# Moving the row split of the last output stores from tiles 58 and 59 to tile 48, in a one-core matmul with bias and residual

## The chip, the cores and the metric

The kernel runs on one core of one Trainium2 chip. The metric is the device time of one execution in microseconds (us). The kernel before was at 210.7 us (median of 3 runs, 210.52 to 210.83) when the prediction was made.

## The reference

```python
# x: (16, 512, 1024), weight: (1024, 768), bias: (768,), residual: (16, 512, 768), all float32
def reference(x, weight, bias, residual):
    return (np.matmul(x, weight) + bias + residual).astype(np.float32)
```

The 8,192 rows of the result are worked on as 64 tiles of 128 rows. The output is 25.17 MB, the inputs 61.88 MB.

## The kernel before

TensorE transposes and multiplies tile after tile, VectorE adds, and SyncE issues all DMA transfers from one list, in order. Each entry waits until what it needs is done. A transfer is shared out over DMA engines; the moment at which the trace records that one engine's share is done is called a landing (16 of them for each plain store of 128 rows). "Engine" with a number below is a DMA engine. The cuts of the code are marked with dots.

```python
# ORDER: kind, group S of 16 tiles, first tile, end tile[, row to cut at]
# x: load of x, r: load of residual, s: store of finished tiles, c: half of the last tile
ORDER = [ ...
 ('r', 2, 6, 16), ('s', 1, 0, 16), ('x', 3, 0, 6), ('r', 3, 0, 7), ('x', 3, 6, 16),
 ('r', 3, 7, 16), ('s', 2, 0, 16), ('s', 3, 0, 10), ('s', 3, 10, 12, 108), ('s', 3, 12, 14),
 ('s', 3, 14, 15), ('c', 3, 15, 0), ('c', 3, 15, 1)]
...
            else:                                    # a store
                n0, nl = (0, N) if kind == "s" else LAST[j1]
                j1 = j1 if kind == "s" else j0 + 1
                edges = [0, *cut, P]                 # P = 128
                for p0, p1 in zip(edges, edges[1:]):
                    K_(nc.sync.dma_start(
                        out=out_d[S, p0:p1, j0:j1, n0:n0 + nl],
                        in_=R[p0:p1, (J * S + j0) % RR:(J * S + j0) % RR + j1 - j0, n0:n0 + nl],
                    ))
```

A store of several tiles has one packet per row of SBUF, of 3,072 bytes times the number of tiles: the three stores of 16 tiles are 384 packets of 49,152 bytes in the trace, the ten-tile store 128 of 30,720. Shared equally, a plain store of 128 rows gives 8 packets to each of the 16 DMA engines, as the packet chains of the prediction have it. The entry `('s', 3, 10, 12, 108)` cuts tiles 58 and 59 into 108 rows and 20 rows, so that the engines carry different amounts: in the trace the 108-row store has 12 landings and the 20-row store 10. Eight of those 10 come 0.44 to 0.48 us, about two 6 KB packets, after one of the 12.

No trace gives an engine's number. The numbers used here are names: 0 to 9 are the ten engines of the 20-row store, 10 and 11 the other two of the 108-row store, 12 to 15 the rest. That rows are shared equally, and that a part with fewer landings always uses the lower names, are assumptions.

So engines 0 to 9 carry 9 + 2 = 11 rows of tiles 58 and 59, engines 10 and 11 carry 9, and engines 12 to 15 none.

Of the kernel before, what the change touches and what calls it, by code (L numbers as in the profile page):

```python
# [32 lines left out]
 ('r', 0, 6, 16), ('x', 0, 14, 16), ('x', 1, 0, 6), ('r', 1, 0, 6), ('x', 1, 6, 16),  # L33
 ('r', 1, 6, 16), ('s', 0, 0, 16), ('x', 2, 0, 6), ('r', 2, 0, 6), ('x', 2, 6, 16),
 ('r', 2, 6, 16), ('s', 1, 0, 16), ('x', 3, 0, 6), ('r', 3, 0, 7), ('x', 3, 6, 16),
 ('r', 3, 7, 16), ('s', 2, 0, 16), ('s', 3, 0, 10), ('s', 3, 10, 12, 108), ('s', 3, 12, 14),
 ('s', 3, 14, 15), ('c', 3, 15, 0), ('c', 3, 15, 1)]
LAST = [(0, 512), (512, 256)]


# [256 lines left out]
```

## Time and profile before

| | before |
|---|---|
| median of the timed runs | 210.7 us |
| the profiled execution | 211.16 us, span 209.4 us |
| last VectorE add ends | 204.48 us |
| last store (128 KB) issued, landed | 204.51, 208.30 us |

The page of the kernel before, some lines of its parts 1, 3 and 4:

```profile
span 209.4 us, 3113 instructions
...
PE 202.3 (97%) x1298; PEld 130.3 (62%) x1298; DVE 104.7 (50%) x140; ACT 66.1 (32%) x69; POOL 115.9 (55%) x72
...
q1 hardware_dynamic: 4766, 87.05, 97.6%
q8 instruction: 10, 0.16, 0.3%
q14 instruction: 4, 0.03, 0.0%
...
PE 92%; DMA 4%; ACT 1%; DVE 1%; SPq 0%; issue 0%
```

TensorE is busy for 97% of the span and the DMA engines for 97.6%. The packets of the two queues that the page calls "instruction" are called fetches here. Those of q8 are ten packets of 16,384 bytes, 17 to 20 us apart. They share engines with the data (all ten begin 3 to 4 ns before the end of a data packet): in the packet records a data packet ends at 196.02 us just where the fetch of 196.01 us begins, and the next data packet follows the fetch at 197.06.

What SyncE waited for from 195 us on (us in total, times, longest):

```profile
SPq L130 <- DVE ro L199: 6.1, 2, 4.4
SPq L292 <- DMA out_dram<-ro: 3.5, 1, 3.5
```

The second line is the end of the kernel: 3.5 us in which nothing is left but stores. The timeline near the end (start, us, engine and line):

```profile
200.44 4.40 SPq L130 DMA_DIRECT2D out_dram<-ro  x4
...
203.25 1.23 DVE L262 TENSOR_TENSOR ro<-psum_o,ro 128x512 f32<-128x512 f32 x2 [0.77 <-PE psum_o L258]
```

The last four transfers are issued from 200.44 us on, each as soon as its tile is added. The same stretch by 2 us windows:

```profile
core 0: us, PE busy (x) PEld busy (x) DVE busy (x) ACT busy (x) POOL busy (x), PEclk, DMA share, GB/s
200.00:202.00 2.00, 2.00 (x14) 1.13 (x12) 0.89 (x2) 0.00 (x0) 0.00 (x0) 1.00 0.73 270
202.00:204.00 2.00, 2.00 (x14) 1.08 (x12) 1.18 (x2) 0.00 (x0) 0.00 (x0) 1.00 1.01 416
204.00:206.00 2.00, 0.02 (x1) 0.00 (x0) 0.42 (x1) 0.00 (x0) 0.00 (x0) 1.00 0.92 365
206.00:208.00 2.00, 0.00 (x0) 0.00 (x0) 0.00 (x0) 0.00 (x0) 0.00 (x0) 1.00 0.25 92
```

The DMA share is 0.73 at 200 to 202 us, when some engines have run dry, and 0.25 after 206 us, when only the late ones still work.

### The profile page before, as it was taken

How to read it: one execution, taken by the hardware profiler on the slowest of the kernel's cores; microseconds unless marked ns; L12 is line 12 of the kernel's file. 1: busy time of each engine (PE TensorE's matmuls, PEld its weight loads, DVE VectorE, ACT ScalarE, POOL GpSimd, SP SyncE). 2: the span in 40 equal slices, each digit the busy share in tenths (PEclk: the TensorE clock that was granted, in tenths of full speed). 3: DMA queues.
4: the chain of work that ended last, by engine and by line, in shares of the span. 5: the costliest groups of instructions: out<-in, count | busy, mean ns of one | idle time of the engine just before them, and what ended most of it. 6: DMA issues, size and time to landing. Idle time of an engine off the chain costs nothing.

```text
span 209.4 us, 3113 instructions
## 1 busy us (share of the span) xinstructions
PE 202.3 (97%) x1298; PEld 130.3 (62%) x1298; DVE 104.7 (50%) x140; ACT 66.1 (32%) x69; POOL 115.9 (55%) x72
## 2 busy tenths in 40 slices
PE   7999999999999999999999999999999999999990
PEld 2455666666666666666666666666666666666650
DVE  0448555445544554554455454645544554554460
ACT  2444513312730371310460083320180065330000
POOL 2100039769999806997049603999009940799200
PEclk9999999999999999999999999999999999999998
DMA  6999999999989899899999999999999999998984
GB/s 232 426 425 429 428 433 457 393 464 410 472 378 495 383 494 415 385 415 444 408 435 479 408 417 474 441 412 390 424 476 399 459 407 449 451 441 384 415 354 166
DMA packets 4780, 87.24 MB, mean 417 GB/s; under 512 B 538, under 2 KB 666, under 8 KB 1694
## 3 DMA queue, kind: packets, MB, share of 16 engines
q1 hardware_dynamic: 4766, 87.05, 97.6%
q8 instruction: 10, 0.16, 0.3%
q14 instruction: 4, 0.03, 0.0%
HBM read 61.88 MB, written 25.17 MB: 416 GB/s over the span
## 4 chain that ended last, share of the span: by engine, by line
PE 92%; DMA 4%; ACT 1%; DVE 1%; SPq 0%; issue 0%
PE psum_o L164 78%; PE pt L157 13%; DMA x_tile<-in_x_dram 4%; PE psum_o L258 1%; ACT xb L146 1%; DVE xt L158 0%; DVE ro L262 0%; SPq L119 0%; SPq L122 0%
## 5 line engine op out<-in xcount | busy, mean ns | idle before, releaser
L164 PE MATMUL psum_o<-w_sb,xt 128*128 128x512 bf16 x1008 | 174.0, 326 | 0.3 <-DVE xt L158 0.3
L164 PEld LDWEIGHTS <-xt 128*128 128x128 bf16 x1008 | 98.5, 98 | 59.0 <-DVE xt L158 0.7
L189 POOL TENSOR_TENSOR ro<-ro,bias_sb 128x768 f32<-128x768 f32 x50 | 88.9, 1822 | 48.0 <-DMA ro<-in_residual_dram 37.4
L149 ACT CAST xb<-x_tile 128x1024 bf16<-128x1024 f32 x60 | 59.7, 1043 | 113.8 <-DMA x_tile<-in_x_dram 62.7
L158 DVE COPY xt<-pt 128x1024 bf16<-128x1024 bf16 x64 | 44.0, 691 | 84.9 <-PE pt L157 84.8
L199 DVE TENSOR_TENSOR ro<-psum_o,ro 128x768 f32<-128x768 f32 x49 | 46.5, 948 | 4.3 <-POOL ro L189 3.2
L185 POOL TENSOR_TENSOR ro<-ro 128x768 f32<-128x768 f32 x14 | 25.0, 1815 | 25.1 <-DMA ro<-in_residual_dram 25.0
L157 PE MATMUL pt<-ident,xb 128*128 128x128 f32 x256 | 38.5, 274 | 0.2 <-ACT xb L146 0.2
L157 PEld LDWEIGHTS pt<-ident,xb 128*128 128x128 f32 x256 | 29.9, 142 | 9.0 <-ACT xb L146 1.1
L195 DVE TENSOR_TENSOR ro<-psum_o,bias_sb 128x768 f32<-128x768 f32 x14 | 13.2, 948 | 0.0
L208 PE MATMUL psum_o<-warm 128*128 128x512 bf16 x12 | 5.3, 632 | 1.2 <-DVE warm_a L204 1.2
L229 ACT CAST w_sb<-ro 128x768 bf16<-128x768 f32 x4 | 3.3, 832 | 3.7 <-DMA ro<-in_weight_dram 3.7
L208 PEld LDWEIGHTS <-warm 128*128 128x128 bf16 x12 | 1.6, 144 | 3.9 <-issue 2.8
L229 POOL CAST w_sb<-ro 128x768 bf16<-128x768 f32 x1 | 0.8, 822 | 5.5 <-DMA ro<-in_weight_dram 5.5
L149 DVE CAST xb<-x_tile 128x1024 bf16<-128x1024 f32 x1 | 0.7, 693 | 4.4 <-DMA x_tile<-in_x_dram 4.4
L146 ACT CAST xb<-x_tile 128x512 bf16<-128x512 f32 x3 | 1.8, 616 | 3.4 <-PE psum_o L164 1.7
L258 PE MATMUL psum_o<-w_sb,xt 128*128 128x512 bf16 (+1 forms) x16 | 2.8, 326 | 0.0
L229 DVE CAST w_sb<-ro 128x768 bf16<-128x768 f32 x3 | 1.7, 558 | 2.0 <-DMA ro<-in_weight_dram 2.0
L147 DVE CAST xb<-x_tile 128x512 bf16<-128x512 f32 x3 | 1.2, 424 | 2.4 <-DMA x_tile<-in_x_dram 2.4
L258 PEld LDWEIGHTS <-xt 128*128 128x128 bf16 x16 | 1.6, 98 | 1.1
L223 PE MATMUL psum_o<-warm 128*128 128x512 bf16 x6 | 1.6, 379 | 0.0
L262 DVE TENSOR_TENSOR ro<-psum_o,ro 128x512 f32<-128x512 f32 (+1 forms) x2 | 1.1, 558 | 0.9 <-PE psum_o L258 0.8
(14 smaller groups left out, 5.1 us busy)
## 6 DMA issues: line engine op xcount, KB each, us to landing
out_dram<-ro SPq DMA_DIRECT2D x3, 6144.0 KB, 34.1
x_tile<-in_x_dram SPq DMA_DIRECT2D x3, 5120.0 KB, 24.1
ro<-in_residual_dram SPq DMA_DIRECT2D x3, 3840.0 KB, 25.2
x_tile<-in_x_dram SPq DMA_DIRECT2D x3, 3072.0 KB, 40.2
ro<-in_residual_dram SPq DMA_DIRECT2D x3, 2304.0 KB, 17.5
x_tile<-in_x_dram SPq DMA_DIRECT2D x4, 1024.0 KB, 8.2
x_tile<-in_x_dram SPq DMA_DIRECT2D x2, 2048.0 KB, 21.0
out_dram<-ro SPq DMA_DIRECT2D x1, 3840.0 KB
```

The lines of the kernel that those rows point to most:

```text
L146: K_(nc.scalar.copy(out=dst[:, 0:K // 2], in_=src[:, 0:K // 2]))
L149: K_((nc.scalar.copy if how == "s" else nc.vector.tensor_copy)(out=dst, in_=src))
L157: K_(nc.tensor.transpose(out=pt[:, q, :], in_=words[:, ts(q, P)], identity=ident))
L158: K_(nc.vector.tensor_copy(out=XT[t % XT_N].rearrange("p q m e -> p (q m e)"), in_=pt.rearrange("p q m -> p (q m)").bitcast(BF16),))
L164: K_(nc.tensor.matmul(PO[t % HEAD][:, n0:n0 + nl], lhsT=XT[t % XT_N][:, q, :, e], rhs=w_sb[:, q, e, n0:n0 + nl], start=(q == 0 and e == 0) ...
L185: K_(nc.gpsimd.tensor_add(out=r, in0=r, in1=tmp(t)))
L189: K_(nc.gpsimd.tensor_add(out=r, in0=r, in1=bias_sb))
L195: K_(nc.vector.tensor_add(out=tmp(t), in0=p, in1=bias_sb))
L199: K_(nc.vector.tensor_add(out=row(t), in0=p, in1=row(t)))
L208: K_(nc.tensor.matmul(PO[0][:, 0:512], lhsT=warm[:, 0:P], rhs=warm, start=True, stop=True))
L229: K_(copy(out=w_sb[:, q, e, :], in_=w_st[:, 2 * q + e, :]))
L258: K_(nc.tensor.matmul(p, lhsT=XT[t % XT_N][:, q, :, e], rhs=w_sb[:, q, e, n0:n0 + nl], start=(q == 0 and e == 0), stop=(q == n_q - 1 and e ...
```

## The change

The intent is to balance the end differently. Tiles 58 and 59 go back to a plain store, so that no engine should run dry. The uneven cut moves to tile 48, which is ready long before its turn (its two parts are issued near 161 us): 100 rows on ten engines (10 each), 28 on fourteen (2 each), none on engines 14 and 15. The stores after it are grouped anew.

```diff
- ('r', 3, 7, 16), ('s', 2, 0, 16), ('s', 3, 0, 10), ('s', 3, 10, 12, 108), ('s', 3, 12, 14),
- ('s', 3, 14, 15), ('c', 3, 15, 0), ('c', 3, 15, 1)]
+ ('r', 3, 7, 16), ('s', 2, 0, 16), ('s', 3, 0, 1, 100), ('s', 3, 1, 9), ('s', 3, 9, 12),
+ ('s', 3, 12, 14), ('s', 3, 14, 15), ('c', 3, 15, 0), ('c', 3, 15, 1)]
```

## The prediction

> **What bounds the kernel.** The page gives TensorE 97% of the 209.4 us span, and the chain of waits is 92% TensorE. The change touches no compute, so the body (to 204 us) cannot move. Only the tail can: the timeline ends the last VectorE add at 204.48 us, and the last 128 KB store is issued at 204.51. The issue list puts its landing 3.8 us later, near 208.3; SyncE waits 3.5 us for it. So stores are still queued when compute ends.
>
> **Who is late.** I chained the DMA packet records (each packet starts where an earlier one ends), which gives 16 engines. All but four of them are busy without a gap from the large store of tiles 32-47 to the end. They differ: the ten-tile store (8 packets of 30,720 bytes, 1.138 us each) ends at 198.8-199.4 us on six engines, 200.2-200.7 on seven, 200.95 on one whose packets took 1.18 us (call it N), 201.97 and 202.10 on two that lost about 1.4 us to one 16 KB instruction fetch each (at 196.0 and 176.0 us; call the second P). [...]
>
> [...] the 108-row store has 12 landings, the 20-row one 10. P's landing is in the first (204.61 us) and not in the second (last 204.07), so P is engine 10 or 11. It got 9 rows of 6,144 bytes (0.2305 us each), and its last packet ends at 207.97, landing 208.30. N (one of 0-9, 11 rows) is next, ending at 207.43, then one at 207.02. Four engines (12-15) got none of tiles 58-59; three of them ran dry before the next store, issued at 200.44, reached them.
>
> **What the change does.** Bytes and issue of the last transfers stay; one transfer is added, issued near 161 us while SyncE idles. Estimated work of an engine between the store of tiles 32-47 and the end, from those packet times (3,072 bytes: 0.118 us):
> - before: engines 0-9 15.4 us, 10-11 14.9, 12-15 12.8 plus idling;
> - after: 0-9 15.2 us (12 rows of tile 48), 10-13 14.0 (2 rows), 14-15 13.8 (none).
>
> So P gains 0.9 us (to about 207.05), N 0.2 us (to about 207.25); the engine hit at 196 us, one of 12-15, ends at about 206.9 instead of 205.8. The latest is then N, 0.7 us earlier than P was. Everything of this lies on the critical path, but it is all there is[...].
>
> **Prediction.** 210.7 - 0.7 = 210.0 us, 209.5 to 210.6 at 8 in 10. Faster by over 2%: 0.01; within 2%: 0.98; slower: 0.01.
>
> **What would show it.** The last VectorE add still ends at 204.5 us; SyncE's last wait falls from 3.5 to about 2.8 us; last landing near 207.6; the landings of the last store span less than before (2.1 us); no engine is dry at 200-202 us, so the DMA share there, now 0.73, is near 0.95; P's last packet is 0.9 us earlier.
>
> **What would make it wrong.** The instruction fetches land on other engines or at other times, so that another engine (one of 0-9) is the late one and gains only 0.2 us; [...] (some 6 KB packets of the 108-row store took up to 0.9 us instead of 0.23); N slower than before; or unprofiled runs without these delays, where balance is different.

"Engine" numbers are the names given above, and how the rows divide over the engines was an assumption; the landing counts (12 and 10 before, 10 and 14 after) fit it.

## The result, and the profile after

The changed kernel took 210.73 us (median of 6 runs, 210.65 to 210.90), the kernel before 210.61 us beside it (6 runs, 210.50 to 210.83). The ratio is 1.0006, 95% interval 0.9993 to 1.0019: no difference. The predicted 0.7 us did not come, and 210.73 lies above the range of 209.5 to 210.6.

Page of the changed kernel:

```profile
span 209.0 us, 3116 instructions
...
q1 hardware_dynamic: 4912, 87.05, 97.8%
q8 instruction: 10, 0.16, 0.3%
```

SyncE's waits, the timeline and the windows of the changed kernel:

```profile
SPq L292 <- DMA out_dram<-ro: 2.9, 1, 2.9
```

```profile
200.63 4.40 SPq L130 DMA_DIRECT2D out_dram<-ro  x4
...
203.44 1.23 DVE L262 TENSOR_TENSOR ro<-psum_o,ro 128x512 f32<-128x512 f32 x2 [0.77 <-PE psum_o L258]
```

```profile
core 0: us, PE busy (x) PEld busy (x) DVE busy (x) ACT busy (x) POOL busy (x), PEclk, DMA share, GB/s
200.00:202.00 2.00, 2.00 (x13) 1.18 (x12) 0.88 (x2) 0.00 (x0) 0.00 (x0) 1.00 0.86 363
202.00:204.00 2.00, 2.00 (x15) 1.18 (x12) 1.23 (x2) 0.00 (x0) 0.00 (x0) 1.00 0.96 396
204.00:206.00 2.00, 0.21 (x2) 0.00 (x0) 0.56 (x2) 0.00 (x0) 0.00 (x0) 1.00 0.88 347
206.00:208.00 2.00, 0.00 (x0) 0.00 (x0) 0.00 (x0) 0.00 (x0) 0.00 (x0) 0.75 0.24 90
```

Between these two traces much went as predicted. The last wait fell from 3.5 to 2.9 us (2.8 predicted). The DMA share at 200 to 202 us rose from 0.73 to 0.86 (near 0.95 predicted). The landings of the last store spread over 1.6 us instead of 2.1. The last landing came at 207.91 us instead of 208.30 (near 207.6 predicted), although the last add ended 0.19 us later. That the wait came out so close is partly luck: the engine that comes last here is not N, as predicted, but 13 (below).

But the execution that was profiled before took 211.16 us, above all six of its timed runs. The one profiled after took 210.80 us and is itself one of its six timed runs. The two traces differ by 0.36 us in time where the medians do not differ. So the question is what the kernel before does in its other executions.

### The profile page after: what moved, and what is told of

The parts are those of the page before. It is cut to its first block, busy times and chain, and to the rows that moved or that the text cites. A ratio compares the mean times of both kernels' runs of the same rounds, so it can differ in the third digit from the quotient of the medians.

```text
span 209.0 us, 3116 instructions
## 1 busy us (share of the span) xinstructions
PE 202.0 (97%) x1298; PEld 130.0 (62%) x1298; DVE 104.6 (50%) x140; ACT 66.1 (32%) x69; POOL 116.0 (55%) x72
## 3 DMA queue, kind: packets, MB, share of 16 engines
q1 hardware_dynamic: 4912, 87.05, 97.8%
## 4 chain that ended last, share of the span: by engine, by line
PE 92%; DMA 4%; DVE 1%; SPq 0%; ACT 0%; issue 0%
PE psum_o L164 78%; PE pt L157 13%; DMA x_tile<-in_x_dram 4%; PE psum_o L258 1%; DVE xt L158 0%; ACT xb L146 0%; DVE ro L262 0%; SPq L119 0%; SPq L122 0%
```

## The experiments

All profiles are read the same way. The packet records of the trace carry no engine number. A packet starts where the one before it on its engine ends, so they can be chained into 16 engines. The groups that carry different row counts then tell which engines a chain may be. In small packets near the end the chains sometimes cross; landings of whole transfers were used as a check.

How many engines each part of a cut uses was assumed in every expectation below, and the shares of the rows with it. The pages bear out the sum of the two parts. The traces of both kernels have on q1, besides the data, one packet of 4 bytes for each engine's share of each transfer (538 in before: 32 transfers of 16, the bias of 4, and 12 + 10). So a cut changes the packets of q1: 4,760 in flat_before, 4,766 in before (12 + 10 - 16 = 6 more); 4,904 in flat_after, 4,912 in after (10 + 14 - 16), 4,912 in k13 and k13x2 (13 + 11 - 16), 4,920 in sham64 (16 + 16 - 16), 4,913 in cut104 (13 + 12 - 16). Ident, drop24, drop24b and both (5,207, 4,877, 4,733, 4,918) fit in the same way, with the rows left out and the stores added counted.

In every profile taken, the time of the profiled execution is 2.8 to 2.9 us more than the last landing (211.16 - 208.30, 209.83 - 207.02, 214.60 - 211.78). The last landing is what counts.

In the diffs of the experiments only the entries that change are printed, not whole lines.

### The two kernels again, and without any cut

```diff
 # flat_after: the changed kernel, tile 48 not cut
-('s', 3, 0, 1, 100)
+('s', 3, 0, 1)
 # flat_before: the kernel before, tiles 58 and 59 not cut
-('s', 3, 10, 12, 108)
+('s', 3, 10, 12)
```

Expected of the kernel before, again:

> The kernel before again, unchanged: a control and a second profile. Theory L (lottery: a 16 KB instruction fetch delays one DMA engine by about 1.4 us, and which engine it is differs from one execution to the next; the first profile of before, 211.16 us, was an unlucky draw): timed ratio 1.000 within 0.001; the profiled execution is near 210.6 us, and the last landing comes 3.0 to 3.5 us after the last VectorE add, not 3.8; the engine that took the fetch at 176 us is not again one of 10 and 11. Rival B (the tail of before is always 3.8 us and the change did shorten it, but its body is 0.2 to 0.5 us longer): the tail is 3.8 us again and the last add ends at 204.5 us or earlier.

Expected of the changed kernel, again:

> The changed kernel again, unchanged. Theory L: ratio to before 1.000 to 1.002, tail from the last add to the last landing 3.0 to 3.5 us, the fetch at 176 us on another engine than in the first profile of it. Rival B: tail 3.2 us as in its first profile, last add again 0.2 us or more later than in the profile of before.

Expected of the changed kernel without a cut:

> The changed kernel with tile 48 as one plain 128-row store, so all 16 engines carry the same rows; the cuts at 49 to 56, 57 to 59, 60 to 61 and 62 stay. By the packet times engines 0 to 9 carry 0.47 us less than in the changed kernel, 10 to 13 0.7 us more, 14 and 15 0.9 us more. Theory L (no engine is known beforehand to be late, so the heaviest late engine decides): faster than the changed kernel by 0.2 to 0.5 us, ratio to before 0.998 or so. Rival F (the fetches always fall on the same high-numbered engines, which the odd rows were made to spare): slower than the changed kernel by 0.4 us or more.

Expected of the kernel before without a cut:

> The kernel before with tiles 58 and 59 as one plain 128-row store. By the packet times engines 0 to 9 carry 0.7 us less than in before, 10 and 11 0.2 us less, 12 to 15 1.8 us more (but they idle before). Theory L: faster than before by 0.2 to 0.7 us, ratio about 0.998. Rival F (fixed late engines among 12 to 15): slower by up to 1 us.

Measured (before beside them: 210.78 us, 11 runs, 210.48 to 211.54):

| run | median us | ratio to before (95%) | last add ends | last landing | two latest of the last store |
|---|---|---|---|---|---|
| before, first profile | | | 204.48 | 208.30 | 207.89, 208.30 |
| rep_before | 210.67 | 0.9992 (0.9977 to 1.0007) | 204.54 | 207.87 | 207.86, 207.87 |
| after, first profile | | | 204.67 | 207.91 | 207.69, 207.91 |
| rep_after | 210.61 | 0.9991 (0.9977 to 1.0006) | 204.96 | 207.97 | 207.60, 207.97 |
| flat_after | 211.20 | 1.0019 (1.0003 to 1.0036) | 204.42 | 208.29 | 208.15, 208.29 |
| flat_before | 211.23 | 1.0017 (1.0003 to 1.0031) | 204.49 | 208.33 | 208.21, 208.33 |

The repeat of the kernel before landed 0.43 us earlier than its first profile. SyncE's last wait in it (195 us on) is 2.7 us, less than the 2.9 us of the changed kernel:

```profile
SPq L292 <- DMA out_dram<-ro: 2.7, 1, 2.7
```

So the first profile was not typical, as theory L had it. But theory L also had the fetch near 176 us on another engine in rep_after than in the first profile of the changed kernel, and it fell on the same one (13, as named below).

The flat kernels contradict the rest of that theory. They were to be faster and are 0.4 us slower by the ratios. So there are engines that are late in most executions, and both cuts spare them. The landings of the last 128 KB store of flat_before, engine by engine in order of time (us, from the trace's landing records), show how many:

```
206.17 206.18 206.21 206.23 206.24 206.27 206.28 206.29 206.37 206.38 206.54 206.67 206.90 206.93 | 208.21 208.33
```

Two engines stand 1.3 us behind all others. In the packet records they are the two (the hit engines from here on) that carried the 16 KB instruction fetches near 176 and 196 us. Such a fetch takes 0.9 to 1.1 us on its engine, and the data packet behind the one at 196 us is 0.37 us longer (1.507 instead of 1.138 us in the first profile): together 1.4 us.

Theory H, formed from this and from the groups of the other profiles: the last two fetches fall in most executions on two engines among 13 to 15. The first profile of before was an exception.

### Which engines, and how much to spare them

```diff
 # k13                                # k13x2: the same cut over two tiles
-('s', 3, 0, 1, 100)                  -('s', 3, 0, 1, 100), ('s', 3, 1, 9)
+('s', 3, 0, 1, 117)                  +('s', 3, 0, 2, 117), ('s', 3, 2, 9)
 # both: also the old cut of 58 and 59
-('s', 3, 1, 9), ('s', 3, 9, 12)
+('s', 3, 1, 10), ('s', 3, 10, 12, 108)
 # ident: three tiles with three cuts, to tell engines apart
-('s', 3, 0, 1, 100), ('s', 3, 1, 9)
+('s', 3, 0, 1, 120), ('s', 3, 1, 2, 126), ('s', 3, 2, 3, 117), ('s', 3, 3, 9)
```

Expected of the 117-row cut of tile 48:

> The changed kernel with tile 48 cut at row 117 instead of 100: 117 rows run on 13 engines (9 each) and 11 rows on 11 (1 each), so engines 13 to 15 carry none of it. Theory H (the last two 16 KB instruction fetches, near 176 and 196 us, fall in most executions on two of the engines 13 to 15, by the groups of rep_before, after and rep_after on 13 and 14; those two engines end last in the flat kernels, at 208.2 and 208.3 us, and all others by 207.1): the two gain 0.94 us over flat_after, the others lose 0.24 us, so the last landing is near 207.4 us and the time near 210.2 us, 0.4 to 0.5 us under both kernels. Rival S (it is the odd row counts themselves that delay[...], whichever engine is spared): no faster than the changed kernel, 210.6 to 210.8 us.

Expected of the same cut over two tiles:

> The same cut over tiles 48 and 49 together (6 KB per row), 50 to 56 as one transfer. Theory H: the two late engines gain 1.9 us over flat_after and are no longer last; the other engines lose 0.47 us and end near 207.6 to 207.9 us: 210.5 to 210.7 us, as in both kernels, slower than k13. Rival (the more is taken off engines 13 to 15 the better): faster than k13.

Expected of both cuts together:

> Tile 48 cut at 100 as in the changed kernel and tiles 58 and 59 cut at 108 as in the kernel before. Engines 0 to 9 then carry 1.2 us more than in the flat kernels, and by Theory H they are the last, near 208.3 to 208.8 us: 211.2 to 211.6 us, as slow as the flat kernels or slower, though each cut alone is 0.5 us faster than none. If the two cuts did add up (rival: each removes its own delay): 210.2 us or less.

Expected of the run that names the engines:

> To name the engines, not for time: tile 48 cut at 120 (15 engines, then 8), tile 49 at 126 (14 engines, then 2), tile 50 at 117 (13 engines, then 11). Engine 15 carries none of the three, 14 only 8 rows of tile 48, 13 also 9 rows of tile 49, 12 and 11 9 rows of each of the last two. Theory H: the packets show the fetch near 176 us on engine 13 and the one near 196 us on engine 14. If instead fetches fall on different engines in every execution, there is no reason for these two.

Measured (before beside them: 210.91 us, 11 runs, 210.61 to 211.39):

| run | median us | ratio to before (95%) | last landing | 6 KB packets from 188.5 us on: summed excess over 0.234 us, longest |
|---|---|---|---|---|
| k13 | 210.76 | 0.9999 (0.9986 to 1.0011) | 208.47 | 0.2 us, 0.265 us |
| k13x2 | 211.96 | 1.0052 (1.0035 to 1.0069) | 209.31 | 6.8 us, 0.885 us |
| both | 213.97 | 1.0139 (1.0117 to 1.016) | 211.78 | 11.6 us, 1.124 us |
| ident (one run) | 212.85 | | 209.92 | 0.2 us, 0.262 us |
| for comparison: flat_before | | | 208.33 | 0.5 us, 0.265 us |
| before, its four profiles | | | | 3.3, 3.8, 3.8, 5.8 us; up to 0.935 us |
| after, first profile | | | 207.91 | 0.4 us, 0.267 us |

The engines are named as expected. In ident the chain with the fetch at 176.57 us ends its part of the store of tiles 32 to 47 at 193.65 us and begins the next large store at 195.68, after 17 rows, which by the assumed shares only engine 13 has. The chain with the last fetch begins it at 192.92, 8 rows after its end at 191.97, which only engine 14 has by them. In all eleven profiles after the first whose groups can tell (three of before, three of after, k13, cut104, drop24, drop24b, ident) the two fetches fit engines 13 and 14. Only ident names both by itself; the groups of before leave 12 to 15, those of k13, cut104 and the two drops 13 to 15.

The times show what the sum of rows left out. k13x2 and both were expected at 210.5 to 210.7 and 211.2 to 211.6 us; they are 1.3 and 2.4 us slower than the upper ends. SyncE's last wait in the run called both (195 us on):

```profile
SPq L292 <- DMA out_dram<-ro: 6.0, 2, 5.7
```

It waits 5.7 us for one landing. The last column of the table says why: some packets of cut stores take two to nearly five times as long as those of plain stores (6 KB). It was more with more bytes per row: the cut at 117 gave an excess of 6.8 us with 6 KB rows (k13x2), and of 0.3 us in the 3 KB packets with 3 KB rows (k13). It was also larger with several cuts: in ident, with three cut 3 KB stores in a row, the 3 KB packets have a summed excess over 0.121 us of 11.0 us (longest 1.30 us), against 0.2 to 0.7 us in the three profiles of the changed kernel with one.

Why those packets are long was not shown: no run tells which rows an engine gets, nor whether the reading or the writing side is slow. That cut stores of 6 KB rows have the long packets (up to 0.885 us in k13x2, 1.124 in both) and plain ones do not (at most 0.267 us in flat_before and after) is shown. It does not take an odd number of rows: drop24b below, with 8 rows of 6 KB on each of 13 engines, still has four packets of 0.51 to 0.68 us and an excess of 2.0 us.

k13 missed too: 210.2 us was expected, 210.76 measured, no better than before and within the 210.6 to 210.8 of its rival S. Its profiled execution was the slowest of its six (211.36 us), so that profile says little of the median, and its packets have little excess. Cut104 below spares the same three engines and came out at 0.9991 of before; the two intervals overlap. What held k13 back stays open.

### Taking rows away

Both runs of this section that drop rows give a wrong result: rows 104 to 127 of the cut tiles are never stored.

```diff
 # drop24 (changed kernel) and drop24b (kernel before): only the first part of the cut is stored
-('s', 3, 0, 1, 100)        -('s', 3, 10, 12, 108)
+('s', 3, 0, 1, 104)        +('s', 3, 10, 12, 104)
-for p0, p1 in zip(edges, edges[1:]):
+for p0, p1 in (list(zip(edges, edges[1:]))[:1] if cut else zip(edges, edges[1:])):
 # sham64: two transfers, but the same work for all engines
-('s', 3, 0, 1, 100)
+('s', 3, 0, 1, 64)
 # cut104: 104 rows on 13 engines, 24 on 12
-('s', 3, 0, 1, 100)
+('s', 3, 0, 1, 104)
```

Expected of the changed kernel with 24 rows of tile 48 left out:

> Wrong result on purpose: as flat_after, but of tile 48 only rows 0 to 103 are stored, which is 8 rows on each of engines 0 to 12, as in a plain store, and none on 13 to 15; the last 24 rows are never written. So three engines lose 0.94 us of work, nobody gains any, and no engine has an odd number of rows. Theory H (engines 13 and 14 alone set the end in the flat kernels, 208.2 to 208.3 us, the others end by 207.1): 0.9 us faster than the flat kernels, about 210.3 us, last landing near 207.4. If the end were set by something else (compute, or all engines together): no faster than 211.0 us.

Expected of the even cut:

> The changed kernel with tile 48 cut at row 64: two transfers as in the changed kernel, but 4 rows on each of the 16 engines in both, so the work of every engine is that of flat_after. The five profiled kernels with a cut tile 48 lost 0.2 to 0.3 us of TensorE time near 166 to 171 us, the other four none or 0.1. Theory H with chance (the late landing of the load of tiles 54 to 63 comes from earlier loads and has nothing to do with the cut): as flat_after, 211.2 us, with the loss near 170 us present or absent. Rival (the extra instruction or transfer itself brings the loss): 211.4 us or more with the loss near 170 us present.

Expected of the cut at 104 with all rows stored:

> The changed kernel with tile 48 cut at row 104: 8 rows on engines 0 to 12, then 24 rows, 2 each, on engines 0 to 11. Engines 13 to 15 carry none, as in k13[...]. Theory H: the two late engines as in k13[...]: 210.4 to 210.7 us, at or slightly under both kernels. Rival S: as the changed kernel or slower.

Expected of the changed kernel, a third time:

> The changed kernel a third time, for the spread between executions. Theory H: last landing 207.9 us within 0.2, engines 13 and 14 hit by the last two fetches, both kernels within 0.1% of each other.

Expected of the kernel before with 24 rows of tiles 58 and 59 left out:

> Wrong result on purpose: the kernel before, with tiles 58 and 59 cut at row 104 and only those rows stored, 8 on each of engines 0 to 12, none on 13 to 15. Against before, engines 0 to 9 lose 3 rows each (0.7 us)[...]; 13 to 15 carry what they carried in before. If in before engines 0 to 9 come last by their 11 rows[...] (Theory H): last landing near 207.1 to 207.4 us instead of 207.9, time about 210.0 to 210.2 us, 0.5 to 0.7 us under before. If before is held by a fetch-hit engine among 13 to 15: no change.

Expected of the kernel before, a third time:

> The kernel before, a third profile. Theory H: near 210.7 us, the last two fetches on two of engines 12 to 15 (none of the 6 KB rows of tiles 58 and 59 on them), last landing 207.8 to 207.9 us on an engine that carries 11 rows. If it is again like the first profile: the fetch near 176 us on an engine with 9 rows, last landing 208.3 us.

Expected of the kernel before, a fourth time:

> The kernel before, a fourth profile, expected as rep_before2.

Measured (before beside the first four: 210.68 us, 9 runs; beside the others: 210.63 us, 9 runs):

| run | median us | ratio to before (95%) | last add ends | last landing |
|---|---|---|---|---|
| drop24 | 210.33 | 0.9983 (0.9971 to 0.9996) | 204.49 | 207.48 |
| sham64 | 211.59 | 1.0042 (1.0028 to 1.0055) | 204.41 | 208.22 |
| cut104 | 210.46 | 0.9991 (0.9978 to 1.0003) | 204.70 | 207.83 |
| rep_after2 | 210.53 | 0.9994 (0.9981 to 1.0006) | 204.30 | 207.55 |
| drop24b | 209.83 | 0.9959 (0.9942 to 0.9976) | 204.48 | 207.02 |
| rep_before2 | 210.74 | 0.9998 (0.998 to 1.0017) | 204.63 | 208.04 |
| rep_before3 (one run) | 210.81 | | 204.47 | 207.92 |

SyncE's last wait from 195 us on, in flat_before, drop24 and drop24b:

```profile
SPq L292 <- DMA out_dram<-ro: 3.4, 1, 3.4
```

```profile
SPq L292 <- DMA out_dram<-ro: 2.6, 1, 2.6
```

```profile
SPq L292 <- DMA out_dram<-ro: 2.1, 1, 2.1
```

Drop24 takes 0.94 us (8 rows of 0.118 us) off engines 13 to 15 and gives nobody more. The last landing is 0.81 us earlier than in flat_after, and the time 0.87 us less by the medians (0.76 us by the two ratios to before). So the two fetch-hit engines do set the end of the flat kernels. They do so in the timed runs and not in the profiles alone: all five of drop24 (210.15 to 210.58 us) are below all six of flat_after (211.07 to 211.47).

Drop24b spares engines 13 to 15 as much as the kernel before does (16 rows of 3 KB each), but engines 0 to 9 carry 8 rows of tiles 58 and 59 instead of 11. It is 0.80 us faster than before. Engines 13 to 15 got nothing more taken off, so what sets the end of the kernel before is the extra rows on engines 0 to 9 and their long packets. The expected gain was 0.5 to 0.7 us. Two limits: the 8 rows are not free of long packets either (above), and drop24b has one transfer less than before. A second transfer may cost something by itself (sham64 below is 0.4 us above flat_after by the medians, in intervals that overlap), so a part of the 0.80 us may be that. Rep_before2 and rep_before3 agree: their last landings are 208.04 and 207.92, and the hit engines carry none of the 108 rows (its last landings, 203.79 and 203.66 us, are too early for them; in the first profile it was 204.61). The landing records also say who is last there. In rep_before the two latest landings of the 20-row store, which only engines 0 to 9 have, are at 204.05 and 204.10 us, and the two latest of the next store at 205.94 and 205.95, as eight packets of 0.2305 us later. It is so in rep_before2 and rep_before3 too (204.00 and 204.25 to 205.91 and 206.11; 203.96 and 204.13 to 205.87 and 205.98).

Sham64 is as slow as the flat kernels, or slower (211.59 us against 211.20 and 211.23; 211.2 us was expected). So two transfers instead of one bring nothing here; only the uneven assignment does. Sham64 was also to clear up a side suspicion. The last add of the changed kernel had ended later than that of before, and the chain of waits places the loss at one transpose near 171 us. Before, then after:

```profile
168.46 2.60 PE psum_o L164 x16
171.06 0.44 PE pt L157 x4
```

```profile
168.45 2.60 PE psum_o L164 x16
171.04 0.64 PE pt L157 x4
```

The same step took 0.62 us in rep_before2, so it happens in the kernel before as well:

```profile
171.02 0.62 PE pt L157 x4
```

It took 0.44 us in rep_after2, and in sham64. So neither kernel always has it. It goes with when the load of tiles 54 to 63 lands (169.25 us in the first profile of before and 169.28 in rep_after2, with 0.44 us; 169.83 in that of after, with 0.64), which was issued at 144 us, before anything differs between the kernels. But that it has nothing to do with the change is not shown. The step takes 0.64 to 0.66 us in seven of the eight profiles with an uneven cut of tile 48 and all its rows stored (all but rep_after2), and over 0.6 us in one of the nine others (rep_before2); that is a lot for chance. Nor does sham64 settle it: its one profile is the fastest of its five executions, and its median of 211.59 us lies where the rival had it (211.4 or more). What makes that load earlier or later stays open.

Rep_after2 landed at 207.55 us, earlier than the 207.7 to 208.1 expected. Cut104 is the best correct version by its median, 210.46 us against 210.68 for before and 210.53 for the changed kernel in the same rounds. Its interval includes 1, so it beats neither for certain.

## Why the prediction was wrong

The table gives, as estimates, what an engine carries more or less than in the flat kernels, from packets of 0.2305 us (6 KB) and 0.118 us (3 KB). In the flat kernels engines 13 and 14 end at 208.2 to 208.3 us and all others by 207.1.

| | engines 0 to 9 | engine 13 | engine 14 | end expected from the sum | last landing measured |
|---|---|---|---|---|---|
| before (later profiles) | +0.69 and long packets | -1.84 | -1.84 | others, 207.8 or later | 207.87, 208.04, 207.92 |
| after | +0.47 | -0.71 | -0.94 | all near 207.3 to 207.6 | 207.91, 207.97, 207.55 |
| drop24 | 0 | -0.94 | -0.94 | 207.1 to 207.4 | 207.48 |
| drop24b | 0 | -1.84 | -1.84 | 207.1 | 207.02 |

Two of the three landings of the changed kernel are 0.3 to 0.4 us later than the sum has them. They are those of the two profiles in which the load of tiles 54 to 63 landed late (169.83 and 170.11 us, against 169.28 in rep_after2); the sum does not explain them.

- **"Only the tail can move; compute is not touched."** Right for compute: no instruction of it changed, and the last add ended at 204.3 to 205.0 us in all profiles of both kernels. Whether a part of that spread (the step near 171 us) comes with the change is open.
- **"P is engine 10 or 11, and gains 0.9 us."** This is the step that failed: which engine is late. It was true of the one execution that was profiled. In the three other profiles of before the fetches near 176 and 196 us fell on two of engines 12 to 15, which before already spares by 1.84 us. There P is not late, and the change has nothing to give it. It even gives engines 13 and 14 about 1 us more to do.
- **"The four engines without rows of tiles 58 and 59 ran dry, and their time is free to use."** The dryness was there and became less (0.73 to 0.86). But two of these engines are the hit ones in every later profile of before, so the slack was the protection they needed.
- **"N gains 0.2 us."** Too small for the typical execution, where engines of the group 0 to 9 are last. They are relieved of 0.22 us of rows (+0.69 to +0.47) and of the long packets: the summed 6 KB excess is 3.3 to 5.8 us in the profiles of before and 0.2 to 0.6 us in those of after. The prediction named the long packets only as a risk for the changed kernel; it did not count them for before.
- **Why the two come out equal.** In before the end is set by engines 0 to 9, in after by engines 13 and 14, with 0 to 9 close behind (in the first profile of after the latest packets end at 207.58, 207.33 and 207.27 us, the first two on engines 13 and 14). Late engines changed places. The gain on one side is about what was given away on the other. For before this rests on drop24b; for after it is read from the packet chains, and no run tests it alone.
- **The size and the base.** From trace to trace the last landing did move by 0.39 us. The prediction took 0.7 us off the median of 210.7, but had worked it out from an execution of 211.16 us, which was already 0.46 us above that median. That excess should have been taken off the gain first.
- **"What would make it wrong"** named the right cause: fetches on other engines than in the profile. It was given too little weight in the range.

How often an execution of before is like the first profile is open. Of the 40 timed runs of before beside the experiments five took 211.1 us or more, but no profile caught one of them.

## What to carry to other kernels

When the expected gain is smaller than the difference between the profiled execution and the median of the timed runs, one profile can't carry the argument: profile the same kernel again, and see whether the same engine is late. A static balance of DMA engines is worth only what the late engines have in common from one execution to the next (here moving the cut gave 210.73 us against 210.61), and every row moved lands on another engine that may then be last. Cutting a store at an uneven row made some of its packets several times longer here (6 KB packets of up to 1.124 us instead of 0.234), so cut where rows are small (here a summed excess of 0.3 us with 3 KB rows in k13, 6.8 us with 6 KB rows in k13x2), and only once (11.0 us with three 3 KB cuts in ident). An instruction fetch was not free for the engine that carried it: 0.9 to 1.1 us for the packet, in the tail 0.37 us more for the next data packet, and in the flat kernels 0.87 us of the kernel's time by the medians (drop24 against flat_after).
